# The opening of a one-core decoder layer: loads on two queues, the first scale as a column, modulation passes and low parts by turns, and projection pieces of even lengths

## The chip, the core and the metric

The kernel runs on one core of a Trainium2 chip. Five engines work side by side, each through its own list of instructions in order: TensorE (PE in the profile, its weight loads PEld), VectorE (DVE), ScalarE (ACT), GpSimd (POOL) and SyncE (SP, which here issues nearly all transfers). They wait for each other on semaphores. The metric is the device time of one launch in microseconds. All arithmetic is in 32-bit floats.

## What is computed

One decoder layer on x (256 rows, 2048 columns) with a condition vector c. Cut to what the change touches:

```python
c_act = silu(c)
mod = c_act @ ada_w + ada_b                  # 2048 -> 6 x 2048
sh1, sc1, g1, sh2, sc2, g2 = split(mod, 6)
h = rms_norm(x, norm1_g) * (1 + sc1) + sh1
proj = h @ w_in + b_in                       # 11264 columns: u, lru gate, q, k, v, two branch gates
# gated recurrence (RG-LRU) on u; sliding-window attention on q, k, v; both projected and gated
x = x + g1 * (merged @ w_o)
h2 = rms_norm(x, norm2_g) * (1 + sc2) + sh2
x = x + g2 * ((silu(gate) * up) @ w_ffn_out)   # gate, up = split(h2 @ w_ffn_in)
out = rms_norm(x, final_g)
```

Each of the six vectors of mod is a product of c_act with a 2048 x 2048 matrix. Every row of w_in needs the element of h with the same index, and that element needs its own scale (sc1) and shift (sh1), so two columns of ada_w.

## The kernel before

**Layout.** x is held transposed, 16 steps of 128 model columns ("kt" 0 to 15) on the partitions and 256 sequence rows along the free side; xT0 to xT3 hold four steps each. A slab is 512 columns of a weight matrix. h is held per step as a high part (rounded to TensorE's fast 32-bit form) and a low part (the rest); weights are split in the same way, and a product is three matmuls: high by high, high by low, low by high (`mm3`, L382 to L384).

**Items.** The weights come in items of 1024 columns per partition, two steps kt of one slab. For item i, `do_load` (L313) has SP fetch it into one of five raw buffers, `do_hi` (L330) has ScalarE round it into one of four hi buffers, and `do_lo` (L342) has VectorE subtract into one of **three** lo buffers. In step i of the program the loads run up to item i+5, the high parts to i+3 and the low parts to i+2. The low part of item i therefore stands in VectorE's list in the step of item i-2 and writes the buffer that item i-3 read.

**Modulation passes.** Scale and shift of a step kt are made on VectorE (`ada_cols`, L532): a 128 x 1024 half row of the transposed ada_w ("aw", 512 KB) is multiplied by the condition row and summed into one column of modc. A step needs four passes, two halves for scale (m = 1) and two for shift (m = 0), then a small instruction at L540. `Halves` issues the aw loads on SP, up to seven ahead (two buffers of its own, five spare). Behind the four passes ScalarE makes the step of h (`h_f32`, L565) and rounds it (L591), and VectorE makes its low part (`h_low`, L570). The normalisation x * 1/rms comes first (`x_norm`, L558, four steps at once). A clock kept by the program while it is written decides between which items a pass is put; where a matmul needs a step of h that is not made yet, `hact` puts all missing passes there, ahead of everything that follows in the list.

**Pieces.** The fourteen slabs of u, lru gate, k, v and q (START) are summed over kt in three pieces. Piece 0 takes all slabs up to a first kt, piece 1 takes them all further, piece 2 takes each to the end at 16; between pieces the sums are kept in acc and added there by VectorE (L609). `cuts` sets how far each slab goes in each piece: the first four slabs take two steps by unsplit matmuls in the opening (`First`, L662), every other end is raised as long as `H_0 + H_US * t` allows, where t grows with the work planned so far. The ends before:

```
piece 0:  2  2  2  2  2  3  3  3  4  4  4  5  5  6
piece 1:  6  7  7  8  8  9  9 10 10 11 12 13 13 14
piece 2: 16 in every slab
```

**Opening.** SP loads the small vectors (vec), the four x tiles, the two halves of the first scale column (ak0, ak1) and the first aw halves and slabs. The sums of squares of x go from ScalarE (L188) through additions on VectorE (L191) to two matmuls with ones per half (ssc, L1611). The scale of kt = 0 is not made by passes: `sum_first` (L213) multiplies ak by the condition vector on TensorE. `keep_warm` (L162) issues matmuls whose result isn't used.

## Time and profile before

| | |
|---|---|
| median of 3 runs | 1539.51 us (1538.14 to 1541.71) |
| profiled execution, its own time | 1538.93 us |
| its span | 1537.2 us |
| TensorE busy | 1520.6 us, 99% |
| VectorE busy | 1367.1 us, 89% |
| ScalarE busy | 866.1 us, 56% |
| granted TensorE clock | 0.999 |

Times in the profile are microseconds from the span's start. A row of the timeline gives start, length, engine, line, operation, output and inputs, shape and count; in brackets stands how long the engine was idle just before and what released it. A row of waits gives the waiting engine and line, what it waited for, the sum, the number and the longest. A row of windows gives the stretch and, for TensorE, its weight loads, VectorE, ScalarE and GpSimd, the busy time with the number of instructions, then the granted clock, the busy share of the transfer engines and GB/s. An fp32 matmul outside the fast form leaves two records.

### The profile page before, as it was taken

How to read it: one execution, taken by the hardware profiler on the slowest of the kernel's cores; microseconds unless marked ns; L12 is line 12 of the kernel's file. 1: busy time of each engine (PE TensorE's matmuls, PEld its weight loads, DVE VectorE, ACT ScalarE, POOL GpSimd, SP SyncE). 2: the span in 40 equal slices, each digit the busy share in tenths (PEclk: the TensorE clock that was granted, in tenths of full speed). 3: DMA queues.
4: the chain of work that ended last, by engine and by line, in shares of the span. 5: the costliest groups of instructions: out<-in, count | busy, mean ns of one | idle time of the engine just before them, and what ended most of it. 6: DMA issues, size and time to landing. Idle time of an engine off the chain costs nothing.

```text
span 1537.2 us, 22418 instructions
## 1 busy us (share of the span) xinstructions
PE 1520.6 (99%) x7979; PEld 1304.8 (85%) x7979; DVE 1367.1 (89%) x1835; ACT 866.1 (56%) x1115; POOL 163.5 (11%) x232
## 2 busy tenths in 40 slices
PE   8999999999999999999999999999999999999997
PEld 7899999998888787888888888888888888888886
DVE  7989989899998888988988889999999999888987
ACT  4754443776865456444445666655665556664664
POOL 0000000000000000000002321033312123321200
PEclk9999999999999999999999999999999999999999
DMA  9999998766897897999999998589998989989983
GB/s 365 364 326 333 339 324 288 233 184 219 281 298 248 268 320 259 368 333 333 376 378 356 350 297 268 165 244 315 299 273 248 268 244 299 283 264 298 268 272 123
DMA packets 138304, 444.72 MB, mean 289 GB/s; under 512 B 16048, under 2 KB 16208, under 8 KB 138192
## 3 DMA queue, kind: packets, MB, share of 16 engines
q1 hardware_dynamic: 112912, 384.02, 71.2%
q0 software_dynamic: 24992, 58.75, 16.1%
q8 instruction: 62, 1.02, 0.3%
q10 hardware_dynamic: 288, 0.52, 0.1%
q14 instruction: 50, 0.41, 0.1%
HBM read 439.02 MB, written 4.21 MB: 288 GB/s over the span
## 4 chain that ended last, share of the span: by engine, by line
PE 96%; DMA 2%; DVE 1%; ACT 0%; issue 0%; SPq 0%; DVEq 0%; ACTq 0%
PE pf L1389 10%; PE f L384 7%; PE f L382 7%; PE f L383 7%; PE wi L384 6%; PE wi L382 6%; PE wi L383 6%; PE wl L382 2%; PE wl L384 2%; PE wl L383 2%; PE wga L384 2%; PE wga L383 2%; PE wgl L383 2%; PE wga L382 2%; PE wo L384 2%; PE wa L383 2%
## 5 line engine op out<-in xcount | busy, mean ns | idle before, releaser
L330 ACT CAST hi<-raw 128x1024 fp32r<-128x1024 f32 (+1 forms) x540 | 532.3, 995 | 460.2 <-PE wi L383 113.2
L342 DVE TENSOR_TENSOR lo<-raw,hi 128x1024 fp32r<-128x1024 f32 (+1 forms) x540 | 612.7, 1150 | 81.9 <-issue 47.5
L384 PE MATMUL wi<-h,lo 128*128 128x256 f32 x800 | 226.6, 283 | 3.4 <-DVE lo L342 3.4
L382 PE MATMUL wi<-h,hi 128*128 128x256 f32 x800 | 227.3, 284 | 0.0
L383 PE MATMUL wi<-h,hi 128*128 128x256 f32 x800 | 226.4, 283 | 0.0
L382 PE MATMUL f<-hi,h 128*128 128x512 f32 x406 | 158.9, 391 | 0.0
L383 PE MATMUL f<-lo,h 128*128 128x512 f32 x406 | 158.0, 389 | 0.0
L384 PE MATMUL f<-hi,h 128*128 128x512 f32 x406 | 158.0, 389 | 0.0
L384 PEld LDWEIGHTS wi<-h,lo 128*128 128x128 f32 x800 | 153.5, 192 | 3.8 <-DVE lo L342 3.8
L382 PEld LDWEIGHTS wi<-h,hi 128*128 128x128 f32 x800 | 153.5, 192 | 0.2
L383 PEld LDWEIGHTS wi<-h,hi 128*128 128x128 f32 x800 | 153.5, 192 | 0.2
L532 DVE CUSTOM_DVE_ANT_0 aw<-aw,crow,vec 128x1024 f32<-128x1024 f32 x95 | 121.1, 1278 | 4.5 <-DMA aw<-in_ada_t_dram 4.5
L532 DVE CUSTOM_DVE_ANT_0 aw<-aw,crow,modc 128x1024 f32<-128x1024 f32 x95 | 121.2, 1279 | 2.7 <-DMA aw<-in_ada_t_dram 2.6
L330 ACT CAST hi<-wy 128x1024 fp32r<-128x1024 f32 x55 | 58.0, 1055 | 72.1 <-PE f L384 30.3
L342 DVE TENSOR_TENSOR lo<-wx,hi 128x1024 fp32r<-128x1024 f32 x55 | 67.2, 1223 | 31.7 <-issue 27.6
L330 ACT CAST hi<-wx 128x1024 fp32r<-128x1024 f32 x55 | 58.0, 1055 | 63.9 <-PE pf L1389 24.3
L384 PEld LDWEIGHTS f<-hi,h 128*128 128x128 f32 x406 | 76.2, 188 | 15.9
L383 PEld LDWEIGHTS f<-lo,h 128*128 128x128 f32 x406 | 76.3, 188 | 15.6
L382 PEld LDWEIGHTS f<-hi,h 128*128 128x128 f32 x406 | 76.2, 188 | 15.6
L447 POOL DMA_DIRECT2D wx<-in_w_f_dram x78 | 69.8, 958 | 87.2 <-DMA wx<-in_w_f_dram 85.6
L443 POOL DMA_DIRECT2D wx<-in_w_f_dram x78 | 45.5, 656 | 275.0 <-DVE lo L342 98.2
L342 DVE TENSOR_TENSOR lo<-wy,hi 128x1024 fp32r<-128x1024 f32 x55 | 67.2, 1223 | 7.1 <-ACT hi L330 4.2
(350 smaller groups left out, 3108.2 us busy)
## 6 DMA issues: line engine op xcount, KB each, us to landing
aw<-in_ada_t_dram SPq DMA_DIRECT2D x190, 512.0 KB, 6.9
raw<-in_w_in_dram SPq DMA_DIRECT2D x164, 512.0 KB, 5.2
raw<-in_w_f_dram SPq DMA_DIRECT2D x137, 512.0 KB, 7.2
wx<-in_w_f_dram POOLq DMA_DIRECT2D x156, 256.0 KB, 8.0
raw<-in_w_f2a_dram SPq DMA_DIRECT2D x36, 512.0 KB, 5.9
raw<-in_w_lru_dram SPq DMA_DIRECT2D x32, 512.0 KB, 4.6
raw<-in_w_att_dram SPq DMA_DIRECT2D x32, 512.0 KB, 5.7
raw<-in_w_o_dram SPq DMA_DIRECT2D x32, 512.0 KB, 7.6
```

The lines of the kernel that those rows point to most:

```text
L330: nc.scalar.copy(hi[:, cs], live[i][0][:, cs])
L342: nc.vector.tensor_tensor(lo[:, cs], raw[:, cs], f32(hi[:, cs]), op=ALU.subtract)
L382: nc.tensor.matmul(ps, lhsT=lh, rhs=rh, start=start, stop=False, skip_group_check=True)
L383: nc.tensor.matmul(ps, lhsT=lh, rhs=rl, start=False, stop=False, skip_group_check=True)
L384: nc.tensor.matmul(ps, lhsT=ll, rhs=rh, start=False, stop=stop, skip_group_check=True)
L443: nc.gpsimd.dma_start(x[:, j * 512:(j + 1) * 512], block(0, 1))
L447: nc.gpsimd.dma_start(got["x"][:, j * 512:(j + 1) * 512], block(j, j), accum_op=ALU.add)
L532: nc.vector.tensor_tensor_reduce(out=r, in0=r, in1=crow[j], op0=ALU.mult, op1=ALU.add, scale=1.0, scalar=dst if j else vec[:, v:v + 1], ac ...
L1389: nc.tensor.matmul(bank(t, n), lhsT=l[:, rows(t)], rhs=w[:, c0:c0 + 512], start=kt == 0 and k == 0, stop=kt == (EARLY - 2 if (t, n) == (1, ...
```

## The change

Six things change, all of them ahead of the sixtieth item or so:

1. **Loads.** vec, xT1 and xT3 are issued by ScalarE, the rest by SP in the order xT0, ak0, xT2, ak1; x is laid out so that each tile is one contiguous block.
2. **Squares.** The last x tile is summed in two halves, and TensorE adds three partial sums in place of two.
3. **First scale.** `sum_first` takes ak as the stationary operand and the condition column as the moving one, so the sum is a column of 128 partitions rather than a broadcast row; the pass that picked the diagonal is dropped. Its second half is cut in two around the matmul of rx.
4. **First h.** x * 1/rms is made before the scale is known, and scale and shift are applied together.
5. **Turns.** The first passes for kt = 2 and 3, the first low parts and the copies of the first slabs' sums (`begin.post`) are interleaved one by one.
6. **Pieces.** `cuts` makes every end even and raises it by two. The ends become

```
piece 0:  2  2  2  2  2  2  2  2  2  2  4  4  4  4
piece 1:  4  4  4  6  6  6  6  6  8  8  8  8  8 10
piece 2: 16 in every slab
```

The three pieces now hold 14, 28 and 66 items where they held 22, 47 and 47, some of them of half size.

```diff
--- before.py
+++ after.py
@@ -133,21 +133,16 @@
         nc.scalar.activation(sp.tile([P, 1], F32, tag="st", name="early"), eps_t, AF.Sqrt)
 
 
+
     vec = const.tile([P, NV], F32, name="vec")
-    nc.sync.dma_start(vec, vecs)
-
-    def load_x(name):
-        ts = []
-        for q in range(4):
-            t = b4(f"{name}{q}")
-            nc.sync.dma_start(t, x_t[:, 4 * q:4 * q + 4, :])
-            ts.append(t)
-        return ts
-
-    xT = load_x("xT")
+    nc.scalar.dma_start(vec, vecs)
+    xT = [b4(f"xT{q}") for q in range(4)]
     first = [b4(f"ak{i}", F32, (NK // 2, P)) for i in range(2)]
-    for i in range(2):
-        nc.sync.dma_start(first[i], ada_k[i])
+    for queue, t, from_ in (
+        (nc.sync, xT[0], x_t[0]), (nc.scalar, xT[1], x_t[1]), (nc.sync, first[0], ada_k[0]), (nc.sync, xT[2], x_t[2]),
+        (nc.scalar, xT[3], x_t[3]), (nc.sync, first[1], ada_k[1]),
+    ):
+        queue.dma_start(t, from_)
     ones = const.tile([P, P], F32, name="ones")
     nc.vector.memset(ones, 1.0)
     eps_t = const.tile([P, 1], F32, name="eps_t")
@@ -184,9 +179,13 @@
 
     def squares(q):
 
-        for h in ((slice(0, 4),) if q < 3 else (slice(0, 2), slice(2, 4))):
-            nc.scalar.activation(sqx[q][:, h, :], xT[q][:, h, :], AF.Square)
         a = sqx[q]
+        if q == 3:
+            for h in range(2):
+                nc.scalar.activation(a[:, 2 * h:2 * h + 2, :], xT[q][:, 2 * h:2 * h + 2, :], AF.Square)
+                nc.vector.tensor_tensor(a[:, 2 * h, :], a[:, 2 * h, :], a[:, 2 * h + 1, :], op=ALU.add)
+            return
+        nc.scalar.activation(a, xT[q], AF.Square)
         for n in (2, 1):
             nc.vector.tensor_tensor(a[:, 0:n, :], a[:, 0:n, :], a[:, n:2 * n, :], op=ALU.add)
         if q in (1, 2):
@@ -206,12 +205,14 @@
     squares(2)
     squares(3)
 
-    sc_ps = wtile("sc_ps")[:, 0, 0:P]
+    sc_ps = wtile("sc_ps")[:, 0, 0:1]
+    b_1 = const.tile([P, 1], F32, name="b_1")
+    nc.vector.tensor_scalar(b_1, vec[:, V_ADA + NK:V_ADA + NK + 1], 1.0, None, op0=ALU.add)
 
     def sum_first(a, b):
         for k in range(a, b):
             nc.tensor.matmul(
-                sc_ps, lhsT=cact[:, k:k + 1].broadcast_to([P, P]), rhs=first[k // 8][:, k % 8, :],
+                sc_ps, lhsT=first[k // 8][:, k % 8, :], rhs=cact[:, k:k + 1],
                 start=k == 0, stop=k == NK - 1,
             )
 
@@ -679,8 +680,9 @@
             row = []
             for n, k0 in enumerate(ends[-1]):
                 k1 = K_FIRST if i == 0 and n < N_F else k0 + 1
-                while not (i == 0 and n < N_F) and k1 < NK and k1 + 1 <= H_0 + H_US * (t + (k1 - k0) * T_PE * 512):
-                    k1 += 1
+                k1 = min(k1 + k1 % 2, NK)
+                while not (i == 0 and n < N_F) and k1 < NK and k1 + 2 <= H_0 + H_US * (t + (k1 - k0) * T_PE * 512):
+                    k1 += 2
                 k1 = NK if i == N_PIECES - 1 else k1
                 t += (k1 - k0) * T_PE * 512
                 row.append(k1)
@@ -1606,45 +1608,41 @@
 
     sum_first(0, NK // 2)
     ssc = mtile("ssc")
-    for t in range(2):
-        for q in (2, 3):
+    sq = (sqx[2][:, 0, :], sqx[3][:, 0, :], sqx[3][:, 2, :])
+    for i, x in enumerate(sq):
+        for t in range(2):
             nc.tensor.matmul(
-                ssc[:, t:t + 1], lhsT=sqx[q][:, 0, rows(t)], rhs=ones[:, 0:1], start=q == 2, stop=q == 3,
+                ssc[:, t:t + 1], lhsT=x[:, rows(t)], rhs=ones[:, 0:1], start=i + t == 0, stop=i == 2,
                 skip_group_check=True,
             )
     rc = sp.tile([P, 2], F32, tag="rc", name="rc")
     nc.scalar.activation(rc, ssc[:, 0:2], AF.Sqrt, bias=eps_t, scale=1.0 / D)
     free(m=1)
-    sum_first(NK // 2, NK)
+    sum_first(NK // 2, NK // 2 + 4)
 
     def until(cols):
         while not cols <= cols_done:
             ada.advance(True)
 
-    ada.advance(True)
-    ada.advance(True)
     nc.vector.reciprocal(rc, rc)
     diag = sqx[0][:, 2, :]
     nc.vector.tensor_scalar(diag[:, rows(0)], ident, rc[:, 0:1], None, op0=ALU.mult)
     nc.scalar.activation(diag[:, rows(1)], ident, AF.Copy, scale=rc[:, 1:2])
+    ada.advance(True)
+    ada.advance(True)
     rx_ps = mtile("rx_ps")[:, 0:S]
     nc.tensor.matmul(rx_ps, lhsT=ones, rhs=diag, start=True, stop=True)
+    sum_first(NK // 2 + 4, NK)
     keep_warm(N_WARM[2])
     rx = sp.tile([P, S], F32, tag="rx", name="rx", bufs=1)
     nc.scalar.copy(rx, rx_ps)
-
-    dst = modc[:, 1, 0:1]
-    nc.vector.tensor_tensor_reduce(
-        out=sqx[0][:, 1, 0:P], in0=sc_ps, in1=ident, op0=ALU.mult, op1=ALU.add, scale=1.0,
-        scalar=vec[:, V_ADA + NK:V_ADA + NK + 1], accum_out=dst,
-    )
-    nc.vector.scalar_tensor_tensor(dst, dst, 1.0, vec[:, V_N1:V_N1 + 1], op0=ALU.add, op1=ALU.mult)
+    x0, dst = xT[0][:, 0, :], modc[:, 1, 0:1]
+    nc.vector.tensor_tensor(x0, x0, rx_ps, op=ALU.mult)
+    until({(0, 0)})
+    nc.vector.scalar_tensor_tensor(dst, sc_ps, b_1, vec[:, V_N1:V_N1 + 1], op0=ALU.add, op1=ALU.mult)
     cols_done.add((1, 0))
-    until({(0, 0)})
-    x0 = xT[0][:, 0, :]
-    nc.vector.scalar_tensor_tensor(x0, x0, dst, rx_ps, op0=ALU.mult, op1=ALU.mult)
     hx[0] = sp.tile([P, S], F32, tag="t2", name="hx0")
-    nc.vector.tensor_scalar(hx[0], x0, modc[:, 0, 0:1], None, op0=ALU.add)
+    nc.vector.tensor_scalar(hx[0], x0, dst, modc[:, 0, 0:1], op0=ALU.mult, op1=ALU.add)
     normed.update((0, 1))
     free(b4=6, m=1)
     for n in range(N_F):
@@ -1662,16 +1660,19 @@
     upto("hi", do_hi, 1)
     upto("lo", do_lo, 1)
     hmod.advance(True)
-    for n in range(2):
-        begin.post(n)
+    begin.post(0)
     upto("hi", do_hi, 2)
+    ada.advance(True)
+    upto("lo", do_lo, 2)
+    begin.post(1)
+    ada.advance(True)
+    ada.advance(True)
+    upto("hi", do_hi, 3)
+    begin.post(2)
+    upto("lo", do_lo, 3)
     until({(0, 2), (1, 2)})
     fetch_to(14)
-    begin.post(2)
     hmod.finish_to(lambda: 2 in h_done)
-    upto("lo", do_lo, 2)
-    upto("hi", do_hi, 3)
-    upto("lo", do_lo, 3)
     begin.post(3)
     clock.update(pe=T_START[0], dve=T_START[1], act=T_START[1])
     halves.spare = lambda: len(halves.got) - halves.own < N_SPARE
@@ -1714,7 +1715,7 @@
     w2 = f("w_ffn_out")[0]
     a_k = ada_w[:, D:D + P].reshape(2, NK // 2, P, P).transpose(0, 2, 1, 3)
     made = {
-        "vecs": vecs, "x_t": f("x")[0].T.reshape(NK, P, S).transpose(1, 0, 2), "x_r": f("x")[0], "ada_k": a_k,
+        "vecs": vecs, "x_t": f("x")[0].T.reshape(4, 4, P, S).transpose(0, 2, 1, 3), "x_r": f("x")[0], "ada_k": a_k,
         "ada_t": a_t,
         "w_in": slabs(f("w_in")[0]), "bv_row": f("b_in")[0, 6656:7168], "bm_row": f("b_in")[0, 7168:], "lru_w": lru,
         "w_lru": slabs(f("w_lru_out")[0]), "w_att": slabs(f("w_attn_out")[0]), "w_o": slabs(f("w_o")[0]),
```

Lines behind the opening move by one (L342 becomes L343, L532 becomes L533, and so on). Four places of the instruction order follow. In them loNN and rawNN are the low part and the raw load of item NN, awNN the NN-th half row of ada_w, hxNN the step kt = NN of h, and the rows "ISA modc" read out the sum of the pass above.

VectorE before, where the last step of h is made (the first slab of the third piece is items 69 to 73):

```order
L342 TENSOR_TENSOR lo69_2541<-raw69_2437,hi69_2507 128x1024
L532 ISA aw61_2476,modc_162<-aw61_2476,crow1_109,modc_162 128x1024
L532 ISA modc_162 128x1
L540 SCALAR_TENSOR_TENSOR modc_162<-modc_162,vec_74 128x1
L342 TENSOR_TENSOR lo70_2575<-raw70_2470,hi70_2539 128x1024
L570 TENSOR_TENSOR h7_170<-hx15_2603,h7_170 128x256
L845 MEMSET mask_2607 128x256
L532 ISA aw62_2511,modc_162<-aw62_2511,crow0_108,vec_74 128x1024
L532 ISA modc_162 128x1
L609 TENSOR_TENSOR acc11_1074<-wi11_6_0_2478,acc11_1074 128x512
L609 TENSOR_TENSOR acc11_1074<-wi11_6_1_2479,acc11_1074 128x512
L342 TENSOR_TENSOR lo71_2622<-raw71_2505,hi71_2573 128x1024
```

One pass stands between two low parts; step 15 of h is complete before the low part of item 71.

VectorE in the changed kernel, in the first slab of its third piece (items 42 to 47), where step 12 of h is made:

```order
L343 TENSOR_TENSOR lo48_1995<-raw48_1886,hi48_1957 128x1024
L559 TENSOR_TENSOR xT3_79<-xT3_79,rx_243 128x1024
L533 ISA aw46_1784,modc_164<-aw46_1784,crow0_108,vec_74 128x1024
L533 ISA modc_164 128x1
L533 ISA aw47_1820,modc_164<-aw47_1820,crow0_108,vec_74 128x1024
L533 ISA modc_164 128x1
L533 ISA aw48_1856,modc_164<-aw48_1856,crow1_109,modc_164 128x1024
L533 ISA modc_164 128x1
L533 ISA aw49_1999,modc_164<-aw49_1999,crow1_109,modc_164 128x1024
L533 ISA modc_164 128x1
L541 SCALAR_TENSOR_TENSOR modc_164<-modc_164,vec_74 128x1
L571 TENSOR_TENSOR h6_171<-hx12_2009,h6_171 128x256
```

Four passes for step 12 stand between the low part of item 48 and that of item 49; four more for step 13 follow before the latter, and eight, for steps 14 and 15, between the low parts of items 49 and 50.

SP in the changed kernel at the same place:

```order
L314 DMA raw50_1955<-in_w_in_dram 128x1024
L314 DMA raw51_1991<-in_w_in_dram 128x1024
L504 DMA aw49_1999<-in_ada_t_dram 128x1024
L504 DMA aw50_2003<-in_ada_t_dram 128x1024
L504 DMA aw51_2006<-in_ada_t_dram 128x1024
L504 DMA aw52_2026<-in_ada_t_dram 128x1024
L504 DMA aw53_2029<-in_ada_t_dram 128x1024
L504 DMA aw54_2032<-in_ada_t_dram 128x1024
L504 DMA aw55_2035<-in_ada_t_dram 128x1024
L314 DMA raw52_2054<-in_w_in_dram 128x1024
```

Seven aw loads follow one another behind the load of item 51; eight more (aw56 to aw63) stand between the loads of items 52 and 53. Before, on SP, they alternated with the weights:

```order
L313 DMA raw54_1979<-in_w_in_dram 128x1024
L313 DMA raw55_1999<-in_w_in_dram 128x1024
L503 DMA aw50_2005<-in_ada_t_dram 128x1024
L313 DMA raw56_2022<-in_w_in_dram 128x1024
L503 DMA aw51_2028<-in_ada_t_dram 128x1024
L313 DMA raw57_2046<-in_w_in_dram 128x1024
L503 DMA aw52_2052<-in_ada_t_dram 128x1024
L313 DMA raw58_2063<-in_w_in_dram 128x1024
L313 DMA raw59_2095<-in_w_in_dram 128x1024
```

No more than one aw load stands between two weight loads there.

VectorE in the opening of the changed kernel, behind the first low part:

```order
L343 TENSOR_TENSOR lo0_322<-raw0_277,hi0_320 128x1024
L559 TENSOR_TENSOR xT0_76<-xT0_76,rx_243 128x512
L533 ISA aw6_288,modc_164<-aw6_288,crow0_108,vec_74 128x1024
L533 ISA modc_164 128x1
L343 TENSOR_TENSOR lo1_333<-raw1_279,hi1_330 128x1024
L533 ISA aw7_290,modc_164<-aw7_290,crow0_108,vec_74 128x1024
L533 ISA modc_164 128x1
L533 ISA aw8_292,modc_164<-aw8_292,crow1_109,modc_164 128x1024
L533 ISA modc_164 128x1
L343 TENSOR_TENSOR lo2_349<-raw2_312,hi2_342 128x1024
```

The low part of item 1 stands behind the first pass for step 2, where before it stood behind all four and behind that step's low part.

## The prediction

> **What bounds the kernel now.** I read the page first, then the waits of TensorE over the whole span, then the timeline of the opening engine by engine, then ten- and twenty-microsecond windows.
>
> ```profile
> span 1537.2 us, 22418 instructions
> PE 1520.6 (99%) x7979; PEld 1304.8 (85%) x7979; DVE 1367.1 (89%) x1835; ACT 866.1 (56%) x1115; POOL 163.5 (11%) x232
> PE 96%; DMA 2%; DVE 1%; ACT 0%; issue 0%; SPq 0%; DVEq 0%; ACTq 0%
> ```
>
> TensorE is busy for 1520.6 of 1537.2 us and makes 96% of the chain that ended last. An edit that leaves TensorE's work alone can win only what TensorE waits. All its named waits are these:
>
> ```profile
> PE wi L384 <- DVE lo L342: 3.4, 2, 2.1
> PE sc_ps L213 <- DMA ak<-in_ada_k_dram: 1.2, 1, 1.2
> PE warm L162 <- DVE eps_t L154: 1.1, 1, 1.1
> PE w L662 <- DVE hx L1647: 1.0, 1, 1.0
> PE w L662 <- ACT hx L565: 0.6, 1, 0.6
> PE c_ps L182 <- DVE crow L177: 0.3, 1, 0.3
> ```
>
> The last lies before 56 us:
>
> ```profile
> 54.52 0.39 PE L384 MATMUL wi<-h,lo 128*128 128x256 f32 x1 [1.28 <-DVE lo L342]
> ...
> 1528.08 0.28 PE L384 MATMUL late<-hi,fl 128*128 128x256 f32 x1
> ```
>
> The second row is TensorE's last product; the 8.8 us from its end to the span's end and these 7.6 us are nearly all its 16.6 us of idling. So every gain must come from the opening: 3.4 + 1.2 + 1.0 + 0.6 = 6.2 us are waits that the change touches. After that TensorE never stops:
>
> ```profile
> 100.00:120.00 20.00, 20.00 (x169) 20.00 (x168) 19.12 (x26) 8.87 (x10) 0.00 (x0) 1.00 0.87 301
> ```
>
> This row (of the twenty-microsecond windows) gives TensorE's pace: 169 products in 20 us, 0.118 us each. A full item of the input projection (two steps of kt, four column blocks, three products) is 24 products, 2.84 us; one step of kt is 1.42 us. VectorE, in the same row, is busy for 19.1 of 20 us: it has no room to catch up.
>
> **The pieces: a new stall.** This term decides. The rule in cuts gave, before, piece ends of 6 to 14 steps after the second piece, so the third began with kt = 6 and much of h behind it. With even lengths the loop asks for two more steps at once, passes its test less often, and the second piece ends at 4, 4, 4, 6, 6, 6, 6, 6, 8, 8, 8, 8, 8, 10. The last piece still runs to 16 in every slab. So its first slab, items 42 to 47 in the new count (14 items of the first piece, 28 of the second), goes from kt = 4 to kt = 15 in 17 us, and needs the whole of h by item 47, where before it was needed by item 73. The modulations are not made earlier. The order rows of VectorE and SP show that: 8 full passes stand between the low parts of items 48 and 49, and 8 more before that of item 50, where before there was one between two low parts.
>
> Per step kt there are four passes (shift and scale, two halves each), then ScalarE's two instructions, then the low part. This sequence stands in VectorE's timeline once without anything between (two of its four passes are left out here):
>
> ```profile
> 30.50 1.23 DVE L342 TENSOR_TENSOR lo<-raw,hi 128x1024 fp32r<-128x1024 f32 x1 [2.03 <-ACT hi L330]
> 31.64 0.68 DVE L558 TENSOR_TENSOR xT<-xT,rx 128x512 f32<-128x512 f32 x1
> 32.24 1.28 DVE L532 CUSTOM_DVE_ANT_0 aw<-aw,crow,vec 128x1024 f32<-128x1024 f32 x1
> ...
> 35.94 1.28 DVE L532 CUSTOM_DVE_ANT_0 aw<-aw,crow,modc 128x1024 f32<-128x1024 f32 x1
> ...
> 38.41 0.42 DVE L570 TENSOR_TENSOR h<-hx,h 128x256 fp32r<-128x256 f32 x1 [1.11 <-ACT h L591]
> 38.75 1.22 DVE L342 TENSOR_TENSOR lo<-raw,hi 128x1024 fp32r<-128x1024 f32 x1
> ```
>
> From it: a low part of an item takes 1.14 (30.50 to 31.64), from the first pass to the end of the low part of h 6.59 (32.24 to 38.83), from one kt's first pass to the next's 6.51 (32.24 to 38.75), from the fourth pass alone to the end 2.89 (35.94 to 38.83).
>
> A low part of item i writes the buffer of item i-3 (three lo tiles), so it waits for TensorE's end of item i-3, and everything behind it on VectorE waits too. Let T44 be the end of item 44. A hand-over from TensorE I take at 0.25 us and one to it at 0.06 (estimates: a product is listed at 0.28 and starts every 0.118, so its end lies 0.16 behind its slot; the hx that ended at 19.82 let TensorE go at 19.88 in the rows further down).
> - Item 45 needs kt = 11: 0.25 + 1.14 (low part of 47) + 2.89 + 0.06 = 4.34, then one step of 1.42. Item 45 ends at T44 + 5.76.
> - Item 46 needs kt = 12: behind the low part of 48 stands the normalisation of four columns of x (128x1024; I take 1.14, a two-operand pass of that size like the low part). 0.25 + 1.14 + 1.14 + 6.59 + 0.06 = 9.18. kt = 13 comes 6.51 later, plus its step 1.42: 17.11.
> - Item 47, behind the low part of 49: 0.25 + 1.14 + 6.59 + 0.06 = 8.04, then 6.51 and 1.42: 15.97.
>
> The sum is 38.84 us in which TensorE does three items, 8.52 us: **30.3 us of waiting**, in five waits of about 2.9, 9.2, 5.1, 8.0 and 5.1 us. Nothing takes it back: behind it TensorE had no idle time to give, and items 48 and 49 have their parts ready, which covers the two accumulator additions and the low part of item 50.
>
> The bounds of this term: below, 24.7 us, if the three items' low parts, the normalisation (4 x 1.14) and the hand-overs (1.06) cost nothing; above, about 34, if each of the 16 passes waits a few tenths for its load. The loads are issued early enough by their rows: seven stand behind the load of item 51, which waits only for item 46's low part, and at the rate of these windows a load of 0.52 MB takes 1.3 us, near the 1.21 of a pass:
>
> ```profile
> 10.00:20.00 10.00, 7.77 (x66) 7.37 (x65) 8.41 (x20) 3.26 (x7) 0.00 (x0) 1.00 1.03 406
> ```
>
> ```profile
> aw<-in_ada_t_dram SPq DMA_DIRECT2D x58, 512.0 KB, 7.0
> ```
>
> **The clock after a wait.** No row shows TensorE after an idle time of 5 to 9 us. The nearest are the start of the program and the 2.1 us wait:
>
> ```profile
> 1.06 2.93 PE L162 MATMUL warm<-ones 128*128 128x128 f32 x12 [1.06 <-DVE eps_t L154]
> ...
> 7.83 3.51 PE L162 MATMUL warm<-ones 128*128 128x128 f32 x30
> ...
> 40.02 0.39 PE L384 MATMUL wi<-h,lo 128*128 128x256 f32 x1 [2.12 <-DVE lo L342]
> 40.25 0.28 PE L382 MATMUL wi<-h,hi 128*128 128x256 f32 x1
> 40.37 0.28 PE L383 MATMUL wi<-h,hi 128*128 128x256 f32 x1
> ```
>
> Six products (two rows of the trace each) took 2.93 us at the start, 0.49 each; fifteen took 3.51, 0.23 each: half speed for about 3 us. After 2.12 us of idling the pace of 0.12 is back within a product. Waits of 5 and 9 us are nearer to the first. Steps 12 and 14 hide a doubling (VectorE is slower there); step 13, before the hand-over to item 49's low part, and step 15 do not. Two times 1.42 to 1.5 is 3.0; the bounds are 0 and 4.5. [...]
>
> **The opening.** The rows of TensorE, and two of VectorE:
>
> ```profile
> 12.55 2.02 PE L213 MATMUL sc_ps<-ak,cact 128*128 128x128 f32 x16 [1.21 <-DMA ak<-in_ada_k_dram]
> 14.41 0.95 PE L1611 MATMUL ssc<-ones,sqx 128*128 128x1 f32 x8
> ...
> 19.88 7.17 PE L662 MATMUL w<-hx,wf 128*128 128x256 f32 x32 [1.02 <-DVE hx L1647]
> 27.62 7.17 PE L662 MATMUL w<-hx,wf 128*128 128x256 f32 x32 [0.57 <-ACT hx L565]
> ```
>
> ```profile
> 17.29 0.35 DVE L1637 CUSTOM_DVE_ANT_0 sqx<-sc_ps,ident,vec 128x128 f32<-128x128 f32 x1 [0.47 <-PE sc_ps L213]
> ...
> 19.47 0.35 DVE L1647 TENSOR_SCALAR hx<-xT,modc 128x256 f32<-128x256 f32 x1
> ```
>
> - First scale as a column: eight products with 128 moving columns took 2.02 us (0.25 each), four with one column 0.95 (0.24 each). The form wins nothing on TensorE. On VectorE it drops the 0.35 us pass and its 0.47 us wait; part of that is on the way to 19.88.
> - Three partial sums of squares in place of two: two more products, 0.48 us on TensorE; one addition of 128x512 fewer on VectorE.
> - Loads on two queues: the same bytes in another order. The first ak moves ahead of two x tiles, so the 1.21 us wait should go, but x tiles come behind it and the squares may end later. Between 10 and 20 us the engines move 406 GB/s and are full; only the first microseconds have room. [...] First products between 18.8 and 20.9: I take 0.5 us earlier, bounds 1.1 earlier and 1 later.
> - Low parts and passes by turns: the low part of item 1 moves ahead of three passes, and the 2.1 us wait goes. What is late next is the low part of item 3: from 31.64, 0.60 + 1.21 + 1.14 + 2.42 + 1.14 + 1.28 + 1.19 + 0.34 + 2.42 + 1.22 is 44.6, while TensorE, with three full items from 34.0, asks at 42.5. So 2.1 of the 3.4 us come back; 1.3 are won. (The terms: x, a pass, the low part of 1, two passes, the low part of 2, a pass with its small step, ScalarE's two, the low part of h, two passes, the low part of 3.)
>
> Together 1.8 us, between 5.7 (6.2 less the added 0.48) and a loss of 1. Fewer half items save fixed time on ScalarE and VectorE, which TensorE hides: nothing, and nothing to pay.
>
> **Sum.** 30.3 + 3.0 - 1.8 = 31.5 us. On the profiled execution (1538.93 with its span of 1537.2) that is 1570.4; the median of 1539.51 stands 0.6 above it: **1571.0 us**.
>
> **Rivals.**
> - *The modulations are ahead after all* (faster): if VectorE ran the passes behind item 48's low part before TensorE needs kt = 12, only the opening counts: 1539.5 less 1.8 to 5.7, about 1536. It decides where the low part of 48 can run some 30 us before item 45 ends; each microsecond less comes back as waiting. For it: TensorE waited for nothing here before. Against: the three lo tiles, and VectorE at 96% in the window above. 7%.
> - *The loads end last* (slower still): six of the loads (for passes 56 to 61) stand behind item 52's load and reuse buffers that passes free. Were each issued only after the pass before it, at the 7.0 us of the row above less 1.21: 6 x 5.8 = 35 us more, 1605; two in flight, 1588. Against: seven are in flight at the start of the burst. 8%.
> - *The clock stays up and the opening gives all*: 30.3 - 5.7, 1564; inside the range.
> - *The even lengths change the order but not the need* (same): only if the third piece began later in TensorE's work; its ends show otherwise. 2%.
>
> **How the numbers follow.** The late modulations have 83%; their own range is 1559 (24.7, no clock loss and 5.7 won in the opening: 19.0 us more) to 1579 (34, 4.5 and 1 lost in the opening: 39.5 more). Outside lie 7% + 2% on the low side and 8% above, so this is the range too. What a measurement of this kernel can tell from no change is about 0.2%, 3 us: faster 0.07, same 0.02, slower 0.91.
>
> **What would show it.**
>
> ```profile
> 222.69 0.43 DVE L570 TENSOR_TENSOR h<-hx,h 128x256 fp32r<-128x256 f32 x1 [0.62 <-ACT h L591]
> 223.12 0.27 DVE L845 MEMSET mask<- 128x256 f32 x1
> ```
>
> These are the last low part of h and the memset behind it. In the profile of the changed kernel they should stand near 200 us (item 45 is reached at about 34 + 45 x 2.84 + 1 = 163, and the burst lasts 37), with TensorE waiting before them for low parts of h in five waits of some 30 us together, and products at half pace behind the longer ones. Near 40 us there should be no wait for the low part of item 1, and one of about 2 us for that of item 3. The forecast is wrong in its main step if TensorE waits for nothing behind item 44, in the loads if the waits are put down to ada_t transfers, and in the opening if the first products start later than 20.9 us.

## The result, and the profile after

The changed kernel takes 1576.97 us (1573.35 to 1579.09); the kernel before, timed beside it, 1540.61. The ratio is **1.0234, with an interval of 1.0217 to 1.0252**: slower by 36 us, inside the range, 6.0 us above the predicted 1571.0 (1.1 of it because the kernel before itself came out at 1540.61, not 1539.51). The profiled execution took 1579.09 us.

The page of the changed kernel, with span, busy times and the slices of TensorE and its clock:

```profile
span 1577.3 us, 22377 instructions
PE 1537.2 (97%) x7983; PEld 1317.4 (84%) x7983; DVE 1366.6 (87%) x1826; ACT 867.5 (55%) x1108; POOL 162.3 (10%) x232
PE   9999669999999999999999999999999999999997
PEclk8999779999999999999999999999999999999999
```

VectorE and ScalarE do the same work as before. TensorE idles 40.1 us where it idled 16.6, and lists 16.6 us more of busy time for practically the same products. Both are seen in the slices: the fifth and sixth, of 39 us each, hold the idling and the low clock, the first a low clock alone.

All named waits of TensorE, changed kernel:

```profile
PE wi L383 <- ACT h L592: 26.4, 5, 8.4
PE c_ps L177 <- DVE crow L172: 2.7, 1, 2.7
PE warm L157 <- DVE eps_t L149: 1.1, 1, 1.1
PE wi L385 <- DVE lo L343: 1.0, 1, 1.0
PE r_ps L1139 <- ACT yo L1136: 0.2, 1, 0.2
```

The first row is new: five waits for h in the input projection. The waits for the first scale's ak and for the first step of h (1.2, 1.0 and 0.6 us before) are gone, and 1.0 is left of the 3.4 us for low parts; in their place stands a wait of 2.7 us for crow, the condition row.

The five waits in TensorE's timeline (the bracket is the idle time just before, and what ended it):

```profile
175.53 0.45 PE L383 MATMUL wi<-h,hi 128*128 128x256 f32 x1 [2.28 <-ACT h L592]
...
187.12 0.58 PE L383 MATMUL wi<-h,hi 128*128 128x256 f32 x1 [8.41 <-ACT h L592]
...
193.54 0.58 PE L383 MATMUL wi<-h,hi 128*128 128x256 f32 x1 [3.25 <-ACT h L592]
...
204.00 0.58 PE L383 MATMUL wi<-h,hi 128*128 128x256 f32 x1 [7.28 <-ACT h L592]
204.46 0.58 PE L384 MATMUL wi<-h,hi 128*128 128x256 f32 x1
204.84 0.41 PE L385 MATMUL wi<-h,lo 128*128 128x256 f32 x1
210.42 0.58 PE L383 MATMUL wi<-h,hi 128*128 128x256 f32 x1 [5.17 <-ACT h L592]
```

VectorE in the same stretch (low parts of items 47, 48 and 49 at L343, low parts of h at L571):

```profile
171.91 1.23 DVE L343 TENSOR_TENSOR lo<-raw,hi 128x1024 fp32r<-128x1024 f32 x1 [0.42 <-PE wi L385]
175.51 0.43 DVE L571 TENSOR_TENSOR h<-hx,h 128x256 fp32r<-128x256 f32 x1 [1.10 <-ACT h L592]
178.74 1.23 DVE L343 TENSOR_TENSOR lo<-raw,hi 128x1024 fp32r<-128x1024 f32 x1 [2.81 <-PE wi L385]
...
187.10 0.42 DVE L571 TENSOR_TENSOR h<-hx,h 128x256 fp32r<-128x256 f32 x1 [1.10 <-ACT h L592]
...
193.52 0.42 DVE L571 TENSOR_TENSOR h<-hx,h 128x256 fp32r<-128x256 f32 x1 [1.10 <-ACT h L592]
196.76 1.23 DVE L343 TENSOR_TENSOR lo<-raw,hi 128x1024 fp32r<-128x1024 f32 x1 [2.81 <-PE wi L385]
...
210.83 0.27 DVE L847 MEMSET mask<- 128x256 f32 x1
```

This is the circle of the prediction: a low part waits for TensorE to free its buffer, the passes stand behind it, and TensorE waits for the h that they make. From the low part of item 47 (171.91) to the first low part of h behind it (175.51 + 0.43) are 4.03 us, as summed; from one step of h to the next 6.42 (187.10 to 193.52; 6.51 predicted).

Five-microsecond windows of the changed kernel (TensorE, its weight loads, VectorE, ScalarE, GpSimd, then granted clock, transfer engines' busy share, GB/s):

```profile
170.00:175.00 5.00, 3.25 (x28) 3.04 (x26) 3.81 (x12) 1.61 (x2) 0.00 (x0) 1.00 0.85 284
175.00:180.00 5.00, 3.17 (x12) 2.60 (x12) 1.68 (x3) 1.49 (x3) 0.00 (x0) 0.57 0.98 356
180.00:185.00 5.00, 0.00 (x0) 0.00 (x0) 5.00 (x8) 0.00 (x0) 0.00 (x0) 0.50 1.03 404
...
200.00:205.00 5.00, 1.00 (x3) 0.78 (x3) 3.89 (x9) 1.00 (x2) 0.00 (x0) 0.50 0.16 62
...
215.00:220.00 5.00, 5.00 (x38) 5.00 (x37) 2.77 (x3) 2.10 (x2) 0.00 (x0) 0.83 0.31 78
```

VectorE is full while TensorE does nothing, and the transfers are not the limit: they fall to 62 GB/s in the second half of the burst. From 175.69 us on the clock stays at 0.50 for the whole burst.

The opening, TensorE of the changed kernel:

```profile
6.65 6.27 PE L177 MATMUL c_ps<-crow,ones 128*128 128x512 f32 x8 [2.66 <-DVE crow L172]
12.76 3.51 PE L157 MATMUL warm<-ones 128*128 128x128 f32 x30
16.11 1.84 PE L214 MATMUL sc_ps<-cact,ak 128*128 128x1 f32 x16
...
21.29 1.20 PE L1634 MATMUL rx_ps<-sqx,ones 128*128 128x256 f32 x2
...
26.12 15.37 PE L663 MATMUL w<-hx,wf 128*128 128x256 f32 x64
```

The first products start at 26.12 where they started at 19.88, and the projection at 41.14 where it started at 34.45: **the opening is later, not earlier**. Between the two profiled executions the account is: 6.7 us later at that point, 2.4 us fewer in waits for low parts, and 35.9 us more in the burst (the distance from the low part of item 47 to that of item 54 is 55.8 us, and at full pace seven items take 19.9). That makes 40.2, and the last product starts 40.2 us later (1568.30 for 1528.08). The profiled execution of the changed kernel is the slowest of its four, so such sums can differ from those in medians by a few microseconds.

### The profile page after: what moved, and what is told of

The parts are those of the page before. It is cut to its first block, busy times and chain, and to the rows that moved or that the text cites. A ratio compares the mean times of both kernels' runs of the same rounds, so it can differ in the third digit from the quotient of the medians.

```text
span 1577.3 us, 22377 instructions
## 1 busy us (share of the span) xinstructions
PE 1537.2 (97%) x7983; PEld 1317.4 (84%) x7983; DVE 1366.6 (87%) x1826; ACT 867.5 (55%) x1108; POOL 162.3 (10%) x232
## 4 chain that ended last, share of the span: by engine, by line
PE 95%; DMA 3%; DVE 1%; ACT 0%; issue 0%; SPq 0%; DVEq 0%; ACTq 0%
PE pf L1391 9%; PE wi L385 6%; PE wi L383 6%; PE wi L384 6%; PE f L385 6%; PE f L383 6%; PE f L384 6%; PE wl L385 2%; PE wgl L383 2%; PE wgl L385 2%; PE wgl L384 2%; PE wl L383 2%; PE wl L384 2%; PE wga L383 2%; PE wa L384 2%; PE wga L384 2%
## 5 line engine op out<-in xcount | busy, mean ns | idle before, releaser
L343 DVE TENSOR_TENSOR lo<-raw,hi 128x1024 fp32r<-128x1024 f32 (+1 forms) x532 | 611.1, 1164 | 107.7 <-issue 47.7
L383 PE MATMUL wi<-h,hi 128*128 128x256 f32 x800 | 231.1, 289 | 26.4 <-ACT h L592 26.4
L384 PE MATMUL wi<-h,hi 128*128 128x256 f32 x800 | 230.1, 288 | 0.0
L383 PEld LDWEIGHTS wi<-h,hi 128*128 128x128 f32 x800 | 156.4, 195 | 28.0 <-ACT h L592 27.8
L384 PEld LDWEIGHTS wi<-h,hi 128*128 128x128 f32 x800 | 156.4, 196 | 1.2 <-DVE h L571 1.0
L533 DVE CUSTOM_DVE_ANT_0 aw<-aw,crow,modc 128x1024 f32<-128x1024 f32 x95 | 120.9, 1278 | 3.5 <-DMA aw<-in_ada_t_dram 3.5
L533 DVE CUSTOM_DVE_ANT_0 aw<-aw,crow,vec 128x1024 f32<-128x1024 f32 x95 | 120.7, 1278 | 0.7 <-DMA aw<-in_ada_t_dram 0.6
L343 DVE TENSOR_TENSOR lo<-wx,hi 128x1024 fp32r<-128x1024 f32 x55 | 67.2, 1222 | 35.2 <-issue 29.3
L385 PEld LDWEIGHTS f<-hi,h 128*128 128x128 f32 x406 | 76.2, 188 | 16.1
L343 DVE TENSOR_TENSOR lo<-wy,hi 128x1024 fp32r<-128x1024 f32 x55 | 67.2, 1222 | 7.5 <-ACT hi L331 4.5
```

The lines of the kernel that those rows point to most:

```text
L343: nc.vector.tensor_tensor(lo[:, cs], raw[:, cs], f32(hi[:, cs]), op=ALU.subtract)
L383: nc.tensor.matmul(ps, lhsT=lh, rhs=rh, start=start, stop=False, skip_group_check=True)
L384: nc.tensor.matmul(ps, lhsT=lh, rhs=rl, start=False, stop=False, skip_group_check=True)
L385: nc.tensor.matmul(ps, lhsT=ll, rhs=rh, start=False, stop=stop, skip_group_check=True)
L533: nc.vector.tensor_tensor_reduce(out=r, in0=r, in1=crow[j], op0=ALU.mult, op1=ALU.add, scale=1.0, scalar=dst if j else vec[:, v:v + 1], ac ...
```

## Experiments

Two theories of the prediction were to be tested: the late modulations carry the loss (against: the opening does, or the clock), and they come from the third piece beginning before h is there. What had not been foreseen, the later opening, was to be explained. Three causes could make it: the late condition vector, the column form, the new places of the squares.

### The even cuts alone, and the rest alone

The kernel before with the new rule in `cuts` and nothing else:

```diff
+                k1 = min(k1 + k1 % 2, NK)
-                while ... and k1 < NK and k1 + 1 <= H_0 + H_US * (...):
-                    k1 += 1
+                while ... and k1 < NK and k1 + 2 <= H_0 + H_US * (...):
+                    k1 += 2
```

> The kernel before with the even piece ends and nothing else. If the late modulations carry the loss: 1575 us (35 more than before), with waits of TensorE for steps 11 to 15 of h between 160 and 205 us that sum to 24 to 28 us and TensorE at half clock there. If the opening carries most of it: below 1560.

And the changed kernel with the old rule in those lines:

> The change with the piece ends of before. If the late modulations carry the loss and the opening lost some 4 us: 1543 to 1547, no wait of TensorE for h behind 70 us, first products of the opening near 26 us and half clock from 18 to 28 us as in the changed kernel. If the opening, the turns or the loads carry more than that: above 1555. If the opening wins as forecast: below 1540.

The even cuts alone: 1572.3 us (1570.93 to 1574.15), 1.0216 (1.0197 to 1.0235). The waits of TensorE are 26.4 us in five for h, as in the changed kernel, and the burst (low part of item 47 to that of 54) takes 54.4 us. The rest alone: 1541.77 (1539.82 to 1543.24), 1.0016 (1.0007 to 1.0025), a loss of 2.8 us whose interval leaves out zero, with no wait for h and no wait for a low part. So 33 of the 36 us belong to the cuts, and about 3 to the opening.

### The burst's gaps filled with matmuls

The changed kernel with unused matmuls ahead of the late steps of h (their result is not read); it tells the waiting from the clock.

```diff
+    FILL = {11: 7, 12: 34, 13: 18, 14: 29, 15: 18}
     def hact(kt):
+        late = kt not in h_done
         ...
+        if late and kt in FILL:
+            keep_warm(FILL.pop(kt))
```

> The change, with 106 matmuls whose result is not used put on TensorE ahead of steps 11 to 15 of h, so that TensorE works while it waits. If the half clock is a term of its own beside the waiting: the clock stays full from 170 to 220 us, each of these steps takes 1.42 us and the time falls by 5 to 7 us, to about 1571. If the length of the burst on VectorE is all that counts: 1577, no difference.

1571.32 us (1570.08 to 1572.29), 1.0208 (1.0192 to 1.0223): 5.7 us below the changed kernel. Windows of this kernel in the burst:

```profile
180.00:185.00 5.00, 4.10 (x34) 3.71 (x33) 3.90 (x9) 1.00 (x2) 0.00 (x0) 1.00 1.02 402
...
200.00:205.00 5.00, 3.70 (x34) 3.51 (x32) 4.02 (x9) 0.91 (x2) 0.00 (x0) 1.00 0.00 0
205.00:210.00 5.00, 4.78 (x27) 4.58 (x28) 2.26 (x5) 1.14 (x2) 0.53 (x2) 0.70 0.01 3
```

The clock is 1.00 where it was 0.50, but for one window of 3.41 us behind the last wait (207.04 to 210.45, in the last row). The waits for h shrink to 4.2 us in all, and the burst still takes 52.5 us: 32.6 more than at full pace, against 35.9. So holding the clock won 3.3 us in the burst. In the window left at half clock 16 products start, each 0.095 us dearer (worked out below), another 1.5 us. By this estimate the clock is worth 4.8 us of the burst, and the other 31.1 are VectorE's chain of passes, which took as long at either clock (1.28 us a pass at 0.50 in the changed kernel, at 181.02, and 1.28 at 1.00 here, at 192.62). The rest of the 5.7 us is not the work of the edit: in this profile the projection starts at 38.1 us, not 41.1, with the same code ahead of it, so the openings of these two profiles differ by 3.0 us. Compared by their ratios to the kernel before (1.0208 and 1.0234), the two kernels are 4.0 us apart.

### Even ends by another test

The changed kernel with the old test in the new loop (an end is raised by two if one more step is allowed):

```diff
-                while ... and k1 < NK and k1 + 2 <= H_0 + H_US * (...):
+                while ... and k1 < NK and k1 + 1 <= H_0 + H_US * (...):
                     k1 += 2
```

The second piece then ends at 8, 8, 8, 10, 10, 10, 12, 12, 12, 14, 14, 16, 16, 16.

> The change with even ends, but the test of the loop for one more step as before (the ends go to 8, 8, 8, 10, 10, 10, 12, 12, 12, 14, 14, 16, 16, 16 in the second piece). If it is the early need of h and not the evenness that costs: no burst, waits of TensorE at the projection under 2 us, time within 2 us of the run with the old ends, 1542 to 1547. If even pieces cost by themselves: above 1555.

A miss: 1568.52 us (1566.03 to 1569.39), 1.0188 (1.0171 to 1.0204). The burst is gone, and two other waits stand in its place:

```profile
PE wl L383 <- ACT yh L834: 10.7, 1, 10.7
PE wi L383 <- ACT h L592: 6.4, 1, 6.4
```

The first piece now reaches step 3 while it is not made (6.4 us, at 54 us), and the third piece begins late. By the tables the eight slabs of u and lru gate, with which the recurrence can start, are complete after 216 steps, where it was 201 before; the first product behind the recurrence (wl, from yh) waits 10.7 us, up to 489 us. That the one makes the other is read from the tables, not tested by itself. The first wait shows that a first piece can reach too far in kt, the second suggests that a second piece can, too. Of the 29.6 us that this kernel loses 24.7 are accounted for: 17.1 of waits, 2.8 of the opening and 4.8 at half clock behind the two waits (27 products of 256 columns at 0.095 us more each, 11 of 512 columns at 0.20). Another 2.9 are four short waits that the kernel before does not have.

### Odd ends that begin the third piece early

The kernel before with `H_US = 0.058` in place of 0.07: uneven ends as before, but the third piece starts about as early as in the changed kernel.

> The kernel before with one constant changed, H_US 0.058 for 0.07: piece ends of any parity, but the third piece begins after 93 steps as early as in the change (92 there, 138 before). If the early need of h costs: the same burst, TensorE waiting 20 to 30 us for h between 160 and 210 us at half clock, 1565 to 1576 us. If it takes even ends: within 3 us of before.

1575.42 us (1572.33 to 1575.95), 1.0228 (1.0214 to 1.0242), and in its waits:

```profile
PE wi L382 <- ACT h L591: 26.1, 5, 7.3
```

So it isn't the evenness: what counts is how much of h the third piece asks for before VectorE has made it.

### Even ends with an early need avoided

Two tables of even ends, written out in place of `cuts` in the kernel before. Their second pieces are the same; the first kernel has a first piece that goes to 6, the second that of the change:

```diff
-    ends = cuts()
+    ends = [[0] * 14,
+        [2, 2, 2, 2, 2, 2, 4, 4, 4, 4, 4, 4, 6, 6],   # or: 2 2 2 2 2 2 2 2 2 2 4 4 4 4
+        [6, 6, 8, 8, 8, 8, 10, 10, 10, 12, 12, 12, 14, 14], [NK] * 14]
```

> The kernel before with a table of even ends (2 2 2 2 2 2 4 4 4 4 4 4 6 6, then 6 6 8 8 8 8 10 10 10 12 12 12 14 14), so that the third piece begins after as many steps as before (138) and asks for h at nearly the same places. If evenness costs nothing and only the place of the third piece counts: no wait of TensorE for h, none for y, and the time within 2 us of before, 1537 to 1541. If even pieces cost by themselves, as the run with ends up to 16 could be read: above 1550.

> The kernel before with even ends as a table: first piece as in the change (ten slabs to 2, four to 4), second piece as in the balanced run (138 steps). If the 5.9 us wait of the balanced run came from step 3 of h being asked for with step 2 by the seventh slab: the wait is gone, and the time is 1536 to 1540. If even pieces cost by themselves: 1544 or more.

Both missed. The first: 1546.34 (1545.33 to 1549.09), 1.0046 (1.0033 to 1.0058), with one wait of 5.9 us for h at 50 us. The second: 1544.75 (1544.03 to 1545.79), 1.0034 (1.0021 to 1.0046); its one wait for h shrank to 3.4 us and stands at 95 to 98.5 us. Windows of the second kernel around it:

```profile
93.39:96.81 3.42, 1.77 (x15) 1.57 (x14) 3.03 (x4) 1.05 (x1) 0.00 (x0) 1.00 1.00 383
96.81:100.22 3.41, 1.62 (x11) 1.42 (x12) 2.16 (x5) 1.00 (x2) 0.00 (x0) 1.00 1.02 396
100.22:103.63 3.41, 3.41 (x18) 3.41 (x18) 1.61 (x3) 1.04 (x1) 0.00 (x0) 0.50 0.19 76
```

The third row is the price that I had left out of both expectations: 1.7 us after the wait has ended, TensorE falls to half clock for one such window. 16 products start in it, each 0.095 us dearer, together 1.5 us. With the wait of 3.4, and 1.2 for a low part of wgl that the kernel before does not wait for, less 0.6 in waits for the low parts of the opening, that is 5.5 for the measured 5.2 us. In the first of the two, 5.9 us of waiting and 19 products at half clock (1.8 us) make 7.7, with 1.2 for wgl and 1.9 less for low parts 7.0, of 7.1 measured. Even ends can be had without the burst, but these two tables still ask for one step of h too early.

### The opening taken apart

From here on the old cuts stand, and the rest of the change is undone in parts: (a) all loads issued by SP in the old order (vec, xT0 to xT3, ak0, ak1), the column kept; (b) the row form of the first scale, two queues kept; (c) both.

```diff
 (a)                                       (b)
-    nc.scalar.dma_start(vec, vecs)        -   sc_ps, lhsT=first[k // 8][:, k % 8, :], rhs=cact[:, k:k + 1],
+    nc.sync.dma_start(vec, vecs)          +   sc_ps, lhsT=cact[:, k:k + 1].broadcast_to([P, P]), rhs=first[k // 8][:, k % 8, :],
```

> The change with the piece ends of before and the first loads all on SP in the order of before (x still as contiguous tiles, first scale still as a column). If the late vec is one cause of the lost opening: the condition column is ready near 3.3 us where it was 5.6, the c_ps products start near 4.3 and take 3.7 us, the projection starts near 36 where it was 40.2, and the time falls by 2 to 4 us, to 1538 to 1540. If the order of the loads is not a cause: 40 and no difference.

> The change with the piece ends of before and the first scale as a broadcast row of 128 columns as before, two queues kept. If the products of one moving column let the clock fall: the clock stays full from 18 to 28 us, the 16 first products of kt = 0 take 7.2 us where they took over 8, the projection starts near 37.5 where it was 40.2, time 1 to 3 us lower. If the half clock came from the wait at 4 us alone: it stays, and the start moves by under 0.5 us.

> The change with the piece ends of before, one queue and the row sum: of the change only the turns, the squares and the order of the first h are left. If late vec and column are the two causes of the lost opening: the projection starts at 33 to 35 us, as before, without the 3.4 us of waits for low parts, and the time is 1536 to 1538, at or below the kernel before. If the turns or squares cost too: a start behind 36 and no gain on before.

(a) 1539.20 us, 0.9996 (0.9987 to 1.0005). (b) 1539.67 us, 1.0004 (0.9995 to 1.0013). (c) 1538.93 us, 0.9999 (0.9990 to 1.0007). Either part undone takes the loss of 2.8 us away, within what can be measured; with both undone, what is left (turns, squares, first h) wins nothing: its projection starts at 34.1 us, 2.3 us of waits for low parts remain of the 3.4, and 1.7 us of waits that the kernel before does not have stand near 831 us, of a cause that stays open.

The condition vector lands later when two engines issue loads. The activation of it, in ScalarE's timeline of the kernel before, of the changed kernel, and of (a), whose bracket is the wait for vec:

```profile
3.22 0.21 ACT L168 ACTIVATE cact<-vec 128x16 f32<-128x16 f32 x1 [1.20 <-DMA vec<-in_vecs_dram]
```

```profile
5.58 0.22 ACT L163 ACTIVATE cact<-vec 128x16 f32<-128x16 f32 x1 [2.14 <-DMA vec<-in_vecs_dram]
```

```profile
3.23 0.22 ACT L163 ACTIVATE cact<-vec 128x16 f32<-128x16 f32 x1 [1.21 <-DMA vec<-in_vecs_dram]
```

2.4 us, and with them crow, c_ps behind its 2.66 us wait, and everything of TensorE behind that. Undoing the order alone removes them. The other runs agree: the activation starts at 3.2 to 3.3 us in all eight profiles in which SP alone issues the first loads, and at 4.8 to 5.6 in all six with two issuers.

The late condition costs TensorE a second time. The eight records of c_ps take 6.27 us in the changed kernel, and 3.79 in (a):

```profile
4.30 3.79 PE L177 MATMUL c_ps<-crow,ones 128*128 128x512 f32 x8 [0.31 <-DVE crow L172]
```

That is 0.78 us a record for 0.47. Over all profiles c_ps takes 3.70 to 4.95 us in the eight with the early vec, 5.20 to 6.73 in the six with the late one. In the rest alone, where it took 5.40 us, a window behind the wait for crow runs at half clock:

```profile
7.50:10.91 3.41, 3.41 (x5) 1.35 (x4) 3.08 (x6) 2.50 (x3) 0.00 (x0) 0.50 1.03 418
```

The changed kernel has five records of c_ps in 3.41 us as well (8.45 to 11.86), but its profile lists that window with a clock of 1.00: there the lengths of the products and the clock column disagree, and no run shows why.

With the column form the clock fell. Windows of the changed kernel, then of (a), then of (b):

```profile
15.27:18.68 3.41, 3.41 (x33) 3.41 (x33) 1.82 (x6) 0.00 (x0) 0.00 (x0) 1.00 1.05 416
18.68:22.09 3.41, 3.41 (x16) 3.32 (x16) 1.65 (x4) 0.67 (x2) 0.00 (x0) 0.50 1.01 392
22.09:25.51 3.42, 3.42 (x17) 3.33 (x17) 2.17 (x5) 0.71 (x2) 0.00 (x0) 0.50 1.04 398
25.51:28.92 3.41, 3.41 (x11) 2.87 (x11) 3.31 (x7) 0.07 (x1) 0.00 (x0) 0.50 1.04 411
```

```profile
14.76:18.17 3.41, 3.41 (x17) 3.32 (x17) 1.65 (x4) 0.66 (x2) 0.00 (x0) 0.50 1.05 406
...
25.00:28.41 3.41, 3.41 (x17) 3.01 (x16) 2.50 (x7) 0.85 (x2) 0.00 (x0) 1.00 1.03 408
```

```profile
14.00:18.00 4.00, 4.00 (x39) 4.00 (x38) 2.37 (x7) 0.00 (x0) 0.00 (x0) 1.00 1.05 411
18.00:22.00 4.00, 3.95 (x33) 3.71 (x33) 2.90 (x6) 1.04 (x3) 0.00 (x0) 1.00 1.02 401
```

With the column, three windows of 3.41 us run at half clock though TensorE is listed as busy throughout; with the row the clock stays whole. So it is in every profile: two or three such windows between 14 and 30 us in all five kernels with the column, none there in the nine with the row. The products with one moving column take no longer one by one (16 records of sc_ps in 1.84 us, 2.02 with the row before); but behind a stretch of them, 2.6 us in the changed kernel (16.11 to 18.68), comes half clock: rx takes 1.20 us in place of 0.66, five warming matmuls (ten records) 2.48 in place of 1.28, and the first products of the opening start so.

Why (a) and (b) each already come out level, with projections that start at 37.3 and 37.1, some 3 us behind (c)'s 34.1, is in the waits: (a) waits for no low part at all, (b) for 0.2 us, (c) for 2.3, and (b) and (c) each have the 1.7 us near 831, (a) has not. From the first product of the projection to the last one of the kernel TensorE takes 1489.9 us in (a), 1493.7 in (b), 1495.6 in (c) and 1493.6 before. A later TensorE gives VectorE the time that it lacks. An opening later by up to that lead costs next to nothing; the rest alone was later by 5.8 us and paid 2.8.

### The two findings joined

The better table of even ends on top of (c); and the same on (b) with vec issued by SP ahead of all else, to see whether the issuer or the company makes vec late.

> The same table on the run with one queue, the row sum and the turns. If the turns free the low part of item 1 and full first items give VectorE the time: the wait for low parts near 40 us is under 1 us where it was 2.3, time 1535 to 1538, 1 to 3 us below before. If the low part of item 3 is late next, as forecast: a wait of about 2 us there and 1538 to 1540.

> The same table, row sum and turns with x and ak on two queues as in the change, but vec issued first on SP. If only the late vec made the two queues lose: the condition column by 3.5 us, c_ps from 4.5 us, no wait for ak, projection from 33 to 34 us and 1535 to 1538. If two transfers at the start delay vec whoever issues it: cact behind 4.5 us and the projection from 36 or later.

Both missed: 1548.28 us (1546.11 to 1548.84), 1.0054 (1.0042 to 1.0067), and 1546.93 (1544.37 to 1548.35), 1.0046 (1.0032 to 1.0060). Both keep the wait of 3.4 us for h at 96 to 100 us, and in both two windows run at half clock behind it, with 26 products (2.5 us). That explains 7.6 of the 9.4 us that separate the first from (c), with 1.3 for wgl and 0.4 more for low parts. The second settles the question on vec:

```profile
4.84 0.22 ACT L163 ACTIVATE cact<-vec 128x16 f32<-128x16 f32 x1 [1.89 <-DMA vec<-in_vecs_dram]
```

Although SP issues vec first, it is late by 1.6 us as soon as ScalarE starts an x tile beside it, near the 4.94 to 5.58 of the profiles in which ScalarE issues it: the company makes it late, not the issuer. No version beat the kernel before; (a), (b) and (c) equal it.

## Why the prediction was right, and where it was not

**The burst: right in place and mechanism, near in size.** Five waits of TensorE for h at items 45 to 47, no wait put down to ada_t, and the memset behind the last step at 210.83 (near 200 predicted, with an opening 6.7 us later). Predicted were waits of about 2.9, 9.2, 5.1, 8.0 and 5.1, together 30.3 us; listed are 2.28, 8.41, 3.25, 7.28 and 5.17, together 26.4. The difference is not speed won. VectorE's chain sets the pace, and what is listed as TensorE's work fills part of what would have been waiting: a step's first product starts with the high part of h, and the third, which needs the low part, 0.84 us behind it (204.00 to 204.84); the other products run at half clock. The third wait shows it: from one step of h to the next are 6.42 us, the step's twelve products are listed for 3.17 of them (187.12 to 190.29), where a step takes 1.42 at full pace, and 3.25 are left as the wait.

**One step was put in the wrong order, and the last wait came out by luck.** The sum gave step 14 its twelve products ahead of step 15. But item 47 is the last of its slab, and there `products` sorts by column block first (`if b == k1: parts.sort(...)`), so step 15 is needed after three products: those at 204.00, 204.46 and 204.84, and then TensorE waits up to 210.42. That three products at half clock, with the wait for the low part among them, are listed for 1.25 us, near the 1.42 of a whole step, made the last wait 5.17 where 5.1 was foreseen. Nine more products then stand behind the last wait, 1.1 us that the sum lacks: it should have said 31.4 in place of 30.3. The filled burst leaves 31.1.

**The clock: named rightly, sized too small.** From 175.69 to 216.65 the clock is at half, and 66 products start in that stretch. Behind one another they start 0.213 us apart, where it is 0.119 at full clock, so each costs 0.095 us more:

```profile
188.17 0.41 PE L383 MATMUL wi<-h,hi 128*128 128x256 f32 x1
188.38 0.41 PE L384 MATMUL wi<-h,hi 128*128 128x256 f32 x1
```

The waits hide this for steps 12 and 14, as predicted. They do not for steps 11 and 13 and for the 28 products from the last wait to 216.65: 52 products, 4.9 us, and the filled burst gave 3.3 + 1.5 = 4.8. The term had 3.0, and 4.5 as its upper bound. It counted steps 13 and 15 alone, 24 products, and let half clock double a step of 1.42, where twelve products take 1.1 us more. With 1.1 for the order and 1.9 for the clock, the predicted 33.3 become 36.3; the burst took 35.9.

**But one premise of that term was luck.** I read the 2.12 us wait at 40 us as one behind which no clock is lost. The even cuts alone have the same wait, and lose it:

```profile
35.37:38.78 3.41, 1.43 (x12) 1.23 (x11) 2.30 (x5) 2.50 (x5) 0.00 (x0) 1.00 1.03 410
38.78:42.19 3.41, 3.26 (x15) 3.26 (x16) 3.41 (x5) 3.41 (x9) 0.00 (x0) 0.50 1.03 407
```

In the changed kernel the clock fell behind the first wait of 2.28 us, too, so the burst ran at half clock from its start. In the even cuts alone it fell only at 171.90, when step 11 was nearly done, and the burst took 54.4 us in place of 55.8.

**The opening: wrong in sign.** -1.8 us were predicted, within -5.7 and +1; the rest alone measured +2.8. By its own steps:
- *Loads on two queues*: "the 1.21 us wait should go" was right, and so was the doubt about the second queue: the transfer engines are full in either order, with 416 GB/s from 15.27 us in the changed kernel and 406 from 14.76 in (a). What failed is that the only load named as coming behind others was x; vec, the smallest and first needed, was not looked at, and it came 2.4 us later, which put the start of the projection back by 3.0 (37.1 in (b), 34.1 in (c), one profile each). vec came late even where SP issued it first and ScalarE an x tile beside it (4.84 us for 3.2). No run shows the 0.5 us that the sum took for earlier first products: they start at 23.35 in (b) and at 20.04 in (c), 19.88 before.
- *First scale as a column*: "the form wins nothing on TensorE" was right for one product (0.24 against 0.25 us) and wrong for what follows: its three windows at half clock have no term in the sum. With the column, (a) starts the projection 3.2 us later than (c), its like with the row.
- *The squares*: the third partial sum took its 0.48 us and more (12 records in 1.91 us for 8 in 0.95, in part at half clock), and the squares were not late.
- *Turns*: the wait for the low part of item 1 is gone as predicted. The 2.1 us wait foreseen for item 3 came, as 1.1 us, only where the opening was early again (in (c), at 43.9; its other 1.2 us, at 53.9, stood before as 1.3 at 54.5); in the changed kernel TensorE was late enough to need none, but for the 1.0 us at 65.7.
- From 34.45 to 41.14 the start of the projection moved by the later condition (warming ends at 16.1, not 11.3: 4.8), less the wait for ak (1.2), the sums, in part at half clock (10.0 us from the first sum to the first product, in place of 7.3) and the products themselves (0.4): 6.7. By the sign that the prediction named, first products later than 20.9 us, the opening's forecast was plainly wrong: they start at 26.12.

The total, in medians: the cuts were worth 33.4 us (1572.3 less 1538.94) where the sum had 30.3 + 3.0 = 33.3, the rest 2.8 us where it had -1.8. Together that is 36.2, and 36.4 was measured. By the medians, then, the miss is the opening's 4.6 us. But that 33.4 meets 33.3 is partly luck: in the profile of the even cuts alone the burst costs 34.5 us (54.4 less 19.9), and shorter waits in the opening take back about 1. Between the profiled executions of before and after, the burst is 2.6 us above the 33.3, and the opening 4.3 us later (6.7 less 2.4) where 1.8 earlier was predicted.

**The rivals.** "The modulations are ahead after all" and "the even lengths change the order but not the need" fell with the five waits; "the loads end last" fell with 62 GB/s and then none at the end of the burst; "the clock stays up and the opening gives all" was tried in its first half: with the clock kept up for all but one window, the burst still cost 32.6 us.

## What to carry to other kernels

When a schedule is re-cut, follow the operand that is made late, not the items that are counted: ask at which product the whole of it is needed, and what stands in its maker's list until then. A wait of TensorE cost its length and then, here, none to three windows of 3.41 us at half clock (none behind the 2.12 us in the kernel before, one behind the 3.4 in the second table, three around the 6.4 of the even ends by the other test), each at some 1.5 us where it was full of products, and a wait of 2.1 us came out both ways; so compare expected gains of 1 to 3 us with that. The smallest load can be the one that everything waits for, and a matmul of one moving column (0.24 us here) was no cheaper than one of 128 (0.25), and cost what came after it.

## What the runs showed of the hardware

**The stretches at half clock lasted 3.41 us or a multiple of it.** In the changed kernel the granted clock reads 0.50 from 18.68 to 28.92 and from 175.69 to 216.65: 10.24 and 40.96 us, 3 and 12 times 3.413. In other runs it is 3.4 us (100.22 to 103.63) in the second table of even ends, 6.8 (47.86 to 54.68) at the wait of the first, 10.2 (14.76 to 25.00) in the opening of (a), and 3.4 and 37.5 (38.78 to 42.19, 171.90 to 209.45) in the even cuts alone.

**The same wait came with half clock and without.** The wait for a low part near 38 us is 2.13 us long in the even cuts alone (up to 38.93) and 2.15 in the second table (up to 39.35). In the first the clock reads 0.50 from 38.78 on, with 1.97 us of the wait before that time; in the second it stays at 1.00, with 1.57 of the wait before that time and 0.57 behind. Idle time alone does not sort the cases: of the 3.41 us ahead of a fall TensorE idled 2.28 in the changed kernel (175.69), 1.79 in the second table (100.22) and 1.52 in the filled burst (207.04), but 1.64 in a stretch of that length in the second table (93.39 to 96.81) behind which the clock stayed at 1.00.

**Half clock came behind a stretch without idle time, too.** From 15.27 to 18.68 the changed kernel's TensorE is listed as busy for all 3.41 us, three quarters of it with products of one moving column (from 16.11), and from 18.68 the clock reads 0.50. In (b), with the row, it is as busy from 14.00 to 18.00 (4.00 us), and the clock reads 1.00 up to 22.00. What in those products made the difference was not measured apart.
